# Attention in one visit of TensorE per pair of query blocks, with PSUM banks shared out by hand, in a hybrid decoder layer

## The chip, the core and the metric

The kernel runs on one NeuronCore of a Trainium2 chip. The metric is the device time of one execution in microseconds (us), start to end, as the median of several runs. The profile is one execution taken by the hardware profiler; its span reaches from the first to the last instruction of the core. In the profile PE is TensorE, PEld its weight loads, DVE is VectorE, ACT is ScalarE, POOL is GpSimd and SP the engine that issues most DMAs.

## The reference, cut to what matters

One decoder layer on x of 1024 tokens by 1024 features in float32: RMSNorm and one input projection; mixer A, a gated DeltaNet with 4 heads of 128; mixer B, dilated sliding-window attention with 8 heads of 64; an output projection with a residual; RMSNorm and a gated MLP of width 2816 with a short causal convolution; a last RMSNorm. The change is in mixer B and in what runs beside it. Each query sees three sets of keys, and the three softmaxes are merged by their denominators:

```
for window, dil in ((128, 1), (512, 4), (2048, 16)):     # keys t, t-dil, ..., t-window
    num, den, m = band_attention(stride(q), stride(k), stride(v), window // dil)
...
out = sum(exp(m_i - m_all) * num_i) / sum(exp(m_i - m_all) * den_i)
```

## The kernel before, in words

Everything is kept with features on partitions. A matrix product of the layer is done in three float32r products per 128-row step (`mm3`, L203), high part times high, high times low, low times high, so every weight and activation is cast to a high part on ScalarE (`whi`, `xhi`, `ohi`) and its rest is subtracted on VectorE (`wlo`, `xlo`, `olo`).

TensorE's order is made while the kernel is being built. The class `Weave` (L46) holds a list of Python generators, each a stream of work with a level; a generator yields the time for which its next product isn't ready by a model of engine times (`wv.need`, L95), and `Weave.run` (L102) always steps the stream of the lowest level whose time has come. The products get that order by a token (L190 to L201), so TensorE executes it strictly. The order on VectorE and ScalarE is made by a scheduler, which lets the operations through `uv` and `ua` (L151) go ahead of others; it too is fixed before the kernel runs. A product that waits for a bank or an operand therefore holds up all that stands behind it on TensorE.

The streams around the change are these. `dense` (L505) computes the input projection, column block by column block, each in two halves of 512 tokens; a half is 24 products of 128x512 that accumulate in one PSUM bank (`bank("hf")`, L525), and VectorE then scales it out of the bank (`scaled`, L444, into `aqkv` or `xr`). It has the last level and so fills what the others leave. The columns named `a` (queries, keys and values of attention, in four pairs of heads `pi`) go out to DRAM and are loaded again by `att_load` (L877); the columns `z` are gates, which `gate` (L481, `zz` and `og`) applies to the output of mixer A. `out_proj` (L1117) is the output projection, `mixer_splits` (L1089) the casts of its input `ots`.

`attention` (L906) takes a pair of heads at a time, in two groups (`hh`) of four query blocks of 128 tokens. Its unit is a pair of blocks (`u` = 0 and 2, each block an `it`). A block has near keys (its own and the previous block) and, from block 2 on, far keys in four classes by position modulo 4 (`far`, 32 columns per block further back). The steps of a pair are:

- `scores` (L917): per block and head of the pair, one product with the near keys and four small ones with the far keys of the classes. The first block writes the two banks `asc`, the second the two banks `atr`.
- `softmax` and `normalise` (L941): a masked minimum on VectorE, the exponential on ScalarE, a reciprocal and a multiplication on VectorE; the result is `sm`.
- `turn` (L983): transposes of `sm` in halves of 64 rows (`tp_half`, L198), again into `asc` for the first and `atr` for the second block; `turned` (L962) copies them out, the near part on VectorE (`pt`), the far part on ScalarE (`pb`).
- `values` (L1002): products of `pt` with the values, into the bank `po` of the group, one of the two banks `ch`.
- after the second pair of a group, `merge_classes` (L1011): products of `pb` with the values sorted by class, also into `po`; `give` (L1025) copies `po` out (`oT`) on VectorE.

`advance` (L1040) runs these in a pipeline one pair deep: it turns the pair before, then does the scores of the next pair, then the values of the pair before (and its classes). Each of `turn`, `scores`, `values` and `merge_classes` begins with its own `yield`, so that other streams may be placed ahead of it. When `att_values` (L883, transposes of the values of the next head pair) is due, it stands between `turn` and `scores`.

[...] `bank` (L253) draws from four tags of two: `hf`, `atr`, `asc`, `ch`; a tile of a tag waits until the tile two before it has been read by all its readers.

Of the kernel before, what the change touches and what calls it, by code (L numbers as in the profile page):

```python
# [15 lines left out]
P = 128  # L16
# [128 lines left out]
def hybrid_layer(tc, I, out):  # L145
# [16 lines left out]
    pp_ = es.enter_context(tc.tile_pool(name="pp", bufs=2, space=PSUM))  # L162
# [89 lines left out]

    def bank(tag, name="ps"):  # L253
        return tile_(pp_, (P, 512), F32, name, tag, 2)

    def next_bank(tag, *tiles, slack=0.0):

        while max(wv.need(*tiles), wv.slot_free(tag, 2)) + slack > 1e-3:
            yield max(wv.need(*tiles), wv.slot_free(tag, 2)) + slack
        return bank(tag)  # L260
# [218 lines left out]
    put_off = []  # L479

# [24 lines left out]
    def dense():  # L505
# [400 lines left out]
    def attention():  # L906
# [10 lines left out]
        def scores(pair):  # L917

            for it, tag in zip(pair, ("asc", "atr")):
# [4 lines left out]
            yield wv.need(*pair[0]["ps"], *pair[1]["ps"], pair[0]["q"], pair[0]["k"])  # L924
# [37 lines left out]
        def turned(it, h, pts, b, pp):  # L962
# [5 lines left out]
            if it["g"]["pi"] == 3 and it["n"] == 7 and h == 1:  # L968
# [13 lines left out]

        def turn(pair):  # L983
            def wait():

                return max(wv.need(pair[0]["sm"]) + TSLACK[0], *[wv.slot_free(t, n) for t in ("asc", "atr")
                                                                 for n in (1, 2)])
            while wait() > 1e-3:
                yield wait()
# [12 lines left out]
        def values(pair):  # L1002
            yield wv.need(pair[0]["po"], *pair[0]["pt"], slack=-PSLACK)
            for it in pair:
                u = it["u"]
                for i in range(it["n1"] // P):
                    for e, er in enumerate(HALVES):
                        mm(it["po"][er, u * P:(u + 1) * P], v8(it["vn"])[:, it["k0"] // P + i, er],
                           it["pt"][e][:, i * P:(i + 1) * P], 0.11, u == 0 and i == 0, False, skip_group_check=True)
# [30 lines left out]
        def advance(pair, more=None):  # L1040
            done = pipe.pop() if pipe else None
            if done is not None:
                yield from turn(done)
            if more is not None:
                last["values"] = yield from more
            if pair is not None:
                yield from scores(pair)
                pipe.append(pair)
            if done is not None:
                yield from values(done)  # L1050
                if done[1]["u"] == 3:
                    yield from merge_classes(done[0]["g"])
                    give(done[0]["g"])

        for pi in range(4):
            q, k, vn, vc = cur
            for hh in range(2):
# [4 lines left out]
                po = bank("ch")  # L1062
# [6 lines left out]
                g = dict(po=po, pb=pb, nb=nb, hh=hh, pi=pi, vc=vc)  # L1069
                for u in (0, 2):  # L1070
                    more = att_values(qkv[2]) if (hh, u) == (1, 2) and pi < 3 else None
                    yield from advance([dict(n=4 * hh + i, u=i, q=q, k=k, vn=vn, far=32 * max(4 * hh + i - 1, 0), po=po, pb=pb, g=g)
# [3 lines left out]
        yield from advance(None)  # L1076
        wv.done.add("attention")
# [39 lines left out]
    def out_proj():  # L1117
# [6 lines left out]
        todo = [(k, j) for k in range(8) for j in range(2)]  # L1124
        while todo:

            now = [a for a in todo if ("ot", a[0]) in wv.done and (a[1] == 0 or "attention" in wv.done)]
# [3 lines left out]
            k, j = now[0]  # L1131
# [7 lines left out]
            if m not in pts:  # L1139
                pts[m] = [bank(("hf", "ch")[j]) for _ in range(2)]  # L1140
            for h in range(2):
                yield wv.need(pts[m][h], *w, *ots[k])
                mm3(pts[m][h], [t[:, k, :] for t in w], [t[:, half(h)] for t in ots[k]], k == 0, k == 7)
        for j, m in enumerate(MORDER):
            w = ws.pop(0)
            for h in range(2):
# [6 lines left out]
                else:  # L1153
                    pt = pts[m][h]
# [612 lines left out]
```

## Time and profile before

| | us |
|---|---|
| runs, median of 3 (lowest to highest) | 1205.56 (1205.49 to 1207.72) |
| profiled execution, span on the core | 1204.1 |
| median of the runs above that span | 1.46 |
| mean granted TensorE clock | 0.998 |
| attention, from the first scores to the last class values | 308.0 to 463.3 |

The page's part 1 gives busy time per engine and part 4 the chain of work that ended last. A timeline row has the start, the length, the engine and line, and the operation with its tiles, and xN where N like instructions in a row are merged; a float32 product counts as two. Matmuls are pipelined, so lengths of neighbours overlap, and the cost of a step is read from start to start. A windows row has the stretch, its length, then busy time and count for PE, PEld, DVE, ACT and POOL, the granted clock, the DMA share and GB/s. A group row has the total busy time, the mean in ns, and the idle time in front with what ended it. Lines are those of the kernel before; L139 and L141 are the helpers through which VectorE and ScalarE operations are recorded.

### The profile page before, as it was taken

What the parts mean: (1) busy time and instruction counts of PE and PEld (TensorE: products, weight loads), DVE (VectorE), ACT (ScalarE), POOL (GpSimd) and SP (SyncE); (2) the same over time, 40 slices, a digit from 0 to 9 for tenths busy, and PEclk for the clock granted to TensorE, in tenths of its full rate; (3) what the DMA queues carried; (4) which work ended last, traced back from release to release, by engine and by line L of the source; (5) the groups of instructions that cost most, each with busy time, mean ns of one, the idle gap of its engine ahead of it and who ended that gap; (6) DMA issues with size and microseconds to landing.
All of it is one profiled execution on the core that took longest, in us unless ns stands there. A gap on an engine that the chain in (4) does not pass through costs nothing.

```text
span 1204.1 us, 18360 instructions
## 1 busy us (share of the span) xinstructions
PE 1194.7 (99%) x7058; PEld 987.9 (82%) x7058; DVE 957.1 (79%) x1530; ACT 575.9 (48%) x1131; POOL 54.3 (5%) x50
## 2 busy tenths in 40 slices
PE   9999999999999999999999999999999999999997
PEld 7888887898777777888888888888888888888887
DVE  7686985474667687767898989889898889898987
ACT  7383344364444444555554544444454454445452
POOL 0212110023000000000000000000000000000001
PEclk9999999999999999999999999999999999999999
DMA  7323234426433323443123132231322296357734
GB/s 236 106 75 102 77 119 122 157 79 212 166 115 106 106 63 123 150 140 140 56 85 106 59 100 89 69 105 53 105 71 86 94 370 227 109 179 223 242 97 157
DMA packets 81704, 152.72 MB, mean 127 GB/s; under 512 B 21552, under 2 KB 32592, under 8 KB 81616
## 3 DMA queue, kind: packets, MB, share of 16 engines
q1 hardware_dynamic: 80896, 151.02, 38.3%
q8 instruction: 55, 0.90, 0.3%
q10 hardware_dynamic: 720, 0.53, 0.1%
q14 instruction: 33, 0.27, 0.1%
HBM read 113.49 MB, written 35.93 MB: 124 GB/s over the span
## 4 chain that ended last, share of the span: by engine, by line
PE 98%; DVE 1%; ACT 0%; issue 0%; POOL 0%; DVEq 0%; ACTq 0%; POOLq 0%
PE ps L191 48%; PE pa L191 20%; PE dw L191 17%; PE pc L191 10%; PE ps L195 2%; PE ps L200 1%; PE warm L191 0%; DVE x1h L139 0%; ACT sm L141 0%; PE pd L191 0%; DVE sm L141 0%; POOL rs L139 0%; DVE xr L139 0%; ACT u L139 0%; ACT sq L139 0%
## 5 line engine op out<-in xcount | busy, mean ns | idle before, releaser
L191 PE MATMUL dw<-pr 128*128 128x512 f32 (+1 forms) x984 | 211.4, 377 | 0.0
L191 PEld LDWEIGHTS dw<-pr 128*128 128x128 f32 x984 | 176.8, 188 | 33.5
L191 PE MATMUL ps<-xhi,whi 128*128 128x512 f32 x448 | 186.4, 416 | 0.0
L191 PE MATMUL ps<-xhi,wlo 128*128 128x512 f32 x448 | 175.8, 392 | 0.0
L191 PE MATMUL ps<-xlo,whi 128*128 128x512 f32 x448 | 175.4, 391 | 0.0
L191 PE MATMUL pa<-T,pair 128*128 128x512 f32 x528 | 127.1, 390 | 0.1
L191 PEld LDWEIGHTS pa<-T,pair 128*128 128x128 f32 x528 | 99.0, 188 | 20.9 <-ACT u L139 0.5
L191 PEld LDWEIGHTS ps<-xhi,whi 128*128 128x128 f32 x448 | 84.7, 189 | 19.4 <-issue 2.7
L191 PEld LDWEIGHTS ps<-xhi,wlo 128*128 128x128 f32 x448 | 84.3, 188 | 18.4
L191 PEld LDWEIGHTS ps<-xlo,whi 128*128 128x128 f32 x448 | 84.9, 189 | 13.7
L139 ACT ACTIVATE u<-pa 128x512 f32<-128x512 f32 x44 | 26.3, 599 | 109.7 <-PE pa L191 109.7
L139 DVE SCALAR_TENSOR_TENSOR y<-xu,fcw,y 128x1023 f32<-128x1023 f32 (+1 forms) x44 | 56.4, 1281 | 24.4 <-ACT y L139 24.4
L139 ACT ACTIVATE pr<-wd 128x1024 fp32r<-128x1024 f32 x33 | 35.0, 1061 | 73.9 <-DVE wd L139 36.9
L139 ACT ACTIVATE whi<-wst 128x1024 fp32r<-128x1024 f32 (+2 forms) x38 | 38.6, 1015 | 62.7 <-PE ps L191 55.7
L191 PE MATMUL pa<-B,A 128*128 128x512 f32 x264 | 63.5, 390 | 0.0
L191 PE MATMUL pa<-T,S 128*128 128x512 f32 x264 | 63.4, 390 | 0.0
L191 PE MATMUL pc<-T,S 128*128 128x512 f32 x264 | 63.4, 390 | 0.0
L191 PE MATMUL pc<-B,pair 128*128 128x512 f32 x264 | 63.4, 390 | 0.0
L139 DVE TENSOR_TENSOR wst<-wst 128x512 f32<-128x512 f32 x88 | 60.5, 687 | 0.8
L191 PE MATMUL ps<-B,pair 128*128 128x512 f32 x252 | 60.6, 390 | 0.0
L141 ACT ACTIVATE sm<-sm,mx 128x128 f32<-128x128 f32 (+7 forms) x64 | 35.5, 555 | 48.1 <-DVE mx L141 48.1
L191 PEld LDWEIGHTS pa<-T,S 128*128 128x128 f32 x264 | 49.6, 188 | 10.2
(240 smaller groups left out, 2253.1 us busy)
## 6 DMA issues: line engine op xcount, KB each, us to landing
wst<-in_wu SPq DMA_DIRECT2D x44, 512.0 KB, 3.7
wd<-in_wd SPq DMA_DIRECT2D x44, 512.0 KB, 4.5
wst<-in_wi SPq DMA_DIRECT2D x25, 512.0 KB, 3.7
upark<-y SPq DMA_DIRECT2D x22, 512.0 KB, 3.7
r<-upark SPq DMA_DIRECT2D x22, 512.0 KB, 10.2
apark<-aqkv SPq DMA_DIRECT2D x12, 512.0 KB, 3.0
wa<-in_wd SPq DMA_DIRECT2D x22, 256.0 KB, 3.0
wst<-in_wo SPq DMA_DIRECT2D x8, 512.0 KB, 3.8
```

Source lines behind the costliest of these rows:

```text
L139: return getattr(eng, op)(*a, **kw)
L141: return getattr(eng, op)(*a, **kw)
L191: tc.stamp_issue_order_token(nc.tensor.matmul(dst, lhs, rhs, start=start, stop=stop, **kw).ins, TOKEN)
L195: tc.stamp_issue_order_token(nc.tensor.transpose(dst, src, ident).ins, TOKEN)
L200: tc.stamp_issue_order_token(nc.tensor.transpose(dst, src[rows], ident[rows, rows]).ins, TOKEN)
```

## The change

The steps of attention lose their own yields. `ready` waits once ahead of a visit for the softmax of the pair before, for the banks `asc` and `atr`, for the next queries and for `ch`; then turning, next scores, values and classes are placed with nothing between them, and `att_values` comes after the visit. The scores of the first block go to `ch` and of the second to `asc`; the turning keeps `asc` and `atr`. From the start of attention one of the two `hf` banks is `po`, for all groups, and the dense halves alternate between the other `hf` bank and the first `ch` bank (`dense_bank`); no visit is placed while a dense half in that `ch` bank is unfinished (`shared`). At the end of attention `hf` has two banks again, and the next one drawn is the second. `out_proj` works off its first products per half (`h`), and before attention ends only those of the first half of the first output block may be placed.

```diff
+    BANKS = {t: [t + "0", t + "1"] for t in ("hf", "atr", "asc", "ch")}
+    taken = {t: 0 for t in BANKS}
     def bank(tag, name="ps"):
-        return tile_(pp_, (P, 512), F32, name, tag, 2)
+        ring = BANKS[tag]
+        taken[tag] += 1
+        return tile_(pp_, (P, 512), F32, name, ring[(taken[tag] - 1) % len(ring)], 1)
+    def bank_free(tag, n=1):
+        ring = BANKS[tag]
+        return max(wv.slot_free(ring[(taken[tag] + i) % len(ring)], 1) for i in range(n))
...
+    shared, turns_of = [False], [0]
+    def dense_bank():
+        if BANKS["hf"] != ["hf0"]:
+            return bank("hf")
+        turns_of[0] += 1
+        shared[0] = turns_of[0] % 2 == 0
+        return tile_(pp_, (P, 512), F32, "ps", "ch0", 1) if shared[0] else bank("hf")
...
-                pt = bank("hf")
+                pt = dense_bank()
...
+                shared[0] = False
...
-            for it, tag in zip(pair, ("asc", "atr")):
+            for it, tag in zip(pair, ("ch", "asc")):
...
-            yield wv.need(*pair[0]["ps"], *pair[1]["ps"], pair[0]["q"], pair[0]["k"])
...
-            if it["g"]["pi"] == 3 and it["n"] == 7 and h == 1:
+            if it["g"]["pi"] == 3 and it["n"] == 7 and h == 1 and "dense" in wv.done:
...
+        def ready(done, pair):
+            def wait():
+                t = [0.0]
+                if done is not None:
+                    t += [wv.need(done[0]["sm"]) + TSLACK[0], wv.need(done[1]["sm"]) + TSLACK[1],
+                          bank_free("asc", 2), bank_free("atr", 2)]
+                if pair is not None:
+                    t += [wv.need(pair[0]["q"], pair[0]["k"]), bank_free("ch", 2) - (0.7 if done is not None else 0.0)]
+                    if done is None:
+                        t.append(bank_free("asc", 2))
+                return max(t)
+            while wait() > 1e-3 or shared[0]:
+                yield max(wait(), 0.1)
...
         def values(pair):
-            yield wv.need(pair[0]["po"], *pair[0]["pt"], slack=-PSLACK)
+            g = pair[0]["g"]
+            if "po" not in g:
+                g["po"] = bank("po")
...
         def merge_classes(g):
-            yield wv.need(*g["pb"], slack=-PSLACK)
...
         def advance(pair, more=None):
             done = pipe.pop() if pipe else None
+            yield from ready(done, pair)
             if done is not None:
-                yield from turn(done)
-            if more is not None:
-                last["values"] = yield from more
+                turn(done)
             if pair is not None:
-                yield from scores(pair)
+                scores(pair)
                 pipe.append(pair)
             if done is not None:
-                yield from values(done)
+                values(done)
                 if done[1]["u"] == 3:
-                    yield from merge_classes(done[0]["g"])
+                    merge_classes(done[0]["g"])
                     give(done[0]["g"])
+            if more is not None:
+                yield 0.3
+                last["values"] = yield from more
+        BANKS["hf"], BANKS["po"] = ["hf0"], ["hf1"]
+        taken["po"] = 0
...
-                po = bank("ch")
...
         yield from advance(None)
+        BANKS["hf"], taken["hf"] = ["hf0", "hf1"], 1
         wv.done.add("attention")
...
-        todo = [(k, j) for k in range(8) for j in range(2)]
+        todo = [(k, j, h) for k in range(8) for j in range(2) for h in range(2)]
...
-            now = [a for a in todo if ("ot", a[0]) in wv.done and (a[1] == 0 or "attention" in wv.done)]
+            now = [a for a in todo if ("ot", a[0]) in wv.done and (a[1:] == (0, 0) or "attention" in wv.done)]
...
-            if m not in pts:
-                pts[m] = [bank(("hf", "ch")[j]) for _ in range(2)]
+            if (m, h) not in pts:
+                pts[m, h] = bank(("hf", "ch")[j])
```

More of the change, by code (lines that the diff above doesn't have):

```diff
@@ L981, in far_blocks @@
             return [min(4, it["far"] // 32 - 4 * b) for b in range(-(-it["far"] // P))]
-        def turn(pair):
[L984 to L989, printed above, removed]
+        def ready(done, pair):
[11 more added lines that the diff above has]
+                yield max(wait(), 0.1)
+        def turn(pair):
             pts = A("pt", "dv*", shape=(P, 4, 256))
@@ L1068, in attention @@
                     wv.done.add("last group")
-                g = dict(po=po, pb=pb, nb=nb, hh=hh, pi=pi, vc=vc)
+                g = dict(pb=pb, nb=nb, hh=hh, pi=pi, vc=vc)
                 for u in (0, 2):
                     more = att_values(qkv[2]) if (hh, u) == (1, 2) and pi < 3 else None
-                    yield from advance([dict(n=4 * hh + i, u=i, q=q, k=k, vn=vn, far=32 * max(4 * hh + i - 1, 0), po=po, pb=pb, g=g)
+                    yield from advance([dict(n=4 * hh + i, u=i, q=q, k=k, vn=vn, far=32 * max(4 * hh + i - 1, 0), pb=pb, g=g)
                                         for i in (u, u + 1)], more)
@@ L1130, in out_proj @@
                 continue
-            k, j = now[0]
+            k, j, h = now[0]
             todo.remove(now[0])
@@ L1138, in out_proj @@
                 split(raw_weight(I["wo"][MORDER[2]]), *third)
-            if m not in pts:
-                pts[m] = [bank(("hf", "ch")[j]) for _ in range(2)]
-            for h in range(2):
-                yield wv.need(pts[m][h], *w, *ots[k])
-                mm3(pts[m][h], [t[:, k, :] for t in w], [t[:, half(h)] for t in ots[k]], k == 0, k == 7)
+            if (m, h) not in pts:
+                pts[m, h] = bank(("hf", "ch")[j])
+            yield wv.need(pts[m, h], *w, *ots[k])
+            mm3(pts[m, h], [t[:, k, :] for t in w], [t[:, half(h)] for t in ots[k]], k == 0, k == 7)
         for j, m in enumerate(MORDER):
@@ L1153, in out_proj @@
                 else:
-                    pt = pts[m][h]
+                    pt = pts[m, h]
                 ve.tensor_tensor(x1[m][:, half(h)], x1[m][:, half(h)], pt, op=OP.add)
```

8 lines of the change are left out of this document (4 added, 4 removed).

## The prediction

> **What bounds the kernel now.** I read the page's shares first, then its chain of work, then the busy times of the attention stretch beside those of a plain stretch.
>
> ```profile
> PE 1194.7 (99%) x7058; PEld 987.9 (82%) x7058; DVE 957.1 (79%) x1530; ACT 575.9 (48%) x1131; POOL 54.3 (5%) x50
> ...
> PE 98%; DVE 1%; ACT 0%; issue 0%; POOL 0%; DVEq 0%; ACTq 0%; POOLq 0%
> ```
>
> TensorE (PE) is the whole chain. Next, stretches by busy time: attention first, then a stretch of MLP.
>
> ```profile
> 305.77:463.29 157.52, 157.37 (x1727) 121.48 (x1725) 109.71 (x324) 67.89 (x212) 3.65 (x8) 1.00 0.32 103
> 700.00:800.00 100.00, 100.00 (x443) 82.89 (x442) 88.67 (x103) 47.73 (x64) 0.00 (x0) 1.00 0.24 79
> ```
>
> PE never idles in attention: dense products fill every wait. A plain product costs 100/443 = 0.226 us. So only two things can change the time: work or emptying that TensorE no longer does, and waits that it now meets in its own queue with nothing placed before them. VectorE's 109.7 us of 157.5 leave slack on average, not at each moment.
>
> **The change, part by part.** In the profile a turning is L200 sm (T), scores are kT,qT (S), values pt,vn (V), class values pb,vc (C). Before, T and S of one step stand apart with dense products between.
>
> ```profile
> 358.55 0.96 PE L200 MATMUL ps<-ident,sm 64*128 64x64 f32 x24
> 359.44 0.50 PE L191 MATMUL ps<-xhi,whi 128*128 128x512 f32 x1
> ...
> 361.70 1.68 PE L191 MATMUL ps<-kT,qT 64*128 64x256 f32 x40
> ...
> 342.90 1.22 PE L200 MATMUL ps<-ident,sm 64*128 64x64 f32 x32
> 344.04 0.50 PE L191 MATMUL ps<-xhi,whi 128*128 128x512 f32 x1
> ...
> 346.32 0.93 PE L191 MATMUL ps<-kT,qT 64*128 64x128 f32 x8
> 347.18 1.09 PE L191 MATMUL ps<-pt,vn 128*64 128x128 f32 x16
> 348.10 1.51 PE L191 MATMUL ps<-pb,vc 128*64 128x128 f32 x32
> 349.54 0.97 PE L200 MATMUL ps<-ident,sm 64*128 64x64 f32 x12
> ```
>
> Start to start, 24 transposes take 0.89 us, 32 take 1.14 (0.031 each); a short S (blocks 0 and 1) takes 0.86, V 0.92, and the long C 1.44.
>
> *Gain.* From T at 358.55 to S at 361.70 are 3.15 us. Nine products (2.03) and 24 transposes (0.74) explain 2.77; **0.38 us is the price of parting T from S**. It goes if S can follow T with no gap; a T followed directly by S is not in the trace, so the gain is 0 to 0.38. I take 0.33, near the upper end, because T and S load weights of one shape:
>
> ```profile
> 358.54 0.82 PEld L200 LDWEIGHTS ps<-ident,sm 64*128 64x128 f32 x24 [0.35 <-issue]
> ...
> 361.70 0.73 PEld L191 LDWEIGHTS ps<-kT,qT 64*128 64x128 f32 x8 [0.35 <-ACT pb L141]
> ```
>
> The loader idles 0.35 us at each entry from 128-row products into this 64-row shape. [...]
>
> The order of the changed program's instructions shows 16 partings gone (15 T–S, one T–V) and three new ones, where a T now comes apart from the C before it: 16 × 0.33 − 3 × 0.25 = 4.5 us. Three turnings also waited for probabilities:
>
> ```profile
> PEld ps L200 <- DVE sm L141: 0.8, 3, 0.4
> ```
>
> In the changed order 18 or more products stand ahead of a turning, save two places (six and nine). Gain: 4.5 + 0.8 = **5.3 us** (0.8 to 6.2).
>
> *Loss 1, a bank used twice running.* From attention's start "hf" is one bank, hf0, and dense halves alternate between hf0 and ch0. The half in hand at that moment lies in hf0, and the next one again takes hf0. So its first product waits until VectorE has scaled the half just finished. The nearest rows are the last (24th) product of an earlier half and its scaling:
>
> ```profile
> 303.39 0.39 PE L191 MATMUL ps<-xhi,wlo 128*128 128x512 f32 x1
> ...
> 303.82 1.13 DVE L139 TENSOR_TENSOR aqkv<-ps,rstdB 128x512 f32<-128x512 f32 x1 [5.27 <-PE ps L191]
> ```
>
> 0.43 to its start, 1.1 to its end, 0.07 to hand over: 1.6 us where 0.23 was needed. **+1.4 us.** VectorE is free then (bounds 1.2 to 1.7).
>
> *Loss 2, asc inside a visit.* T of a pair's first block writes the two asc banks, and S of the next pair's second block now writes the same two, 0.5 us later in TensorE's own order. It must wait until VectorE has copied the near part (pt) and ScalarE the far part (pb). Before, nine products (2 us) covered that. Unhindered rows:
>
> ```profile
> 367.75 0.96 PE L200 MATMUL ps<-ident,sm 64*128 64x64 f32 x24
> ...
> 368.37 1.42 DVE L141 COPY pt<-ps 128x256 f32<-128x256 f32 x4 [0.50 <-PE ps L200]
> 368.88 1.21 ACT L141 ACTIVATE pb<-ps 96x128 f32<-96x128 f32 x4 [2.54 <-DVE pt L141]
> ```
>
> Copies run at +0.62 us from T's start, one each 0.33; the second pb ends at 1.13 + 0.31 + 0.28 = 1.72. TensorE reaches the fourth local score at 0.89 + 3 × 0.18 = 1.44 (eight loads take 0.73). Wait: 0.28 plus handing over, 0.33. Eight visits (those that turn blocks 2, 3 or 4, 5) pay it: **2.6 us**. The four that turn blocks 0 and 1 have no pb: 0.05 each, **0.2**. Behind the waiting S stand V, C and all dense products. Bounds 0 to 0.6 a visit.
>
> *Loss 3, three visits that turn blocks 6 and 7 ahead of a next pair.* In two of them the program puts on VectorE, right at T, the scaling of the dense half that has just ended, then two copies, then a wlo subtraction, then two copies. Costs:
>
> ```profile
> L139 DVE TENSOR_TENSOR wlo<-wst,whi 128x1024 fp32r<-128x1024 f32 (+2 forms) x38 | 45.5, 1199 | 8.8 <-ACT whi L139 8.6
> ...
> 382.56 1.40 DVE L141 COPY pt<-ps 128x256 f32<-128x256 f32 x4
> 383.00 1.42 ACT L141 ACTIVATE pb<-ps 128x128 f32<-128x128 f32 x8 [2.43 <-DVE pt L141]
> ```
>
> Scaling ends at 1.07, the copies at 1.75, wlo at 2.9, the other copies at 3.6. V's second half would start at 1.14 + 0.86 + 0.46 = 2.46 and starts at 3.65: 1.2 each, 2.4. The third has VectorE free: the second bank is cleared at 2.05 rather than 1.54, 0.5. **+2.9 us** (1 to 4).
>
> *Loss 4, the end of attention.* Count from S of the last pair (blocks 6, 7).
>
> ```profile
> 451.71 1.89 PE L191 MATMUL ps<-kT,qT 64*128 64x256 f32 x40
> 454.56 0.50 PE L191 MATMUL ps<-xhi,whi 128*128 128x512 f32 x1
> ...
> 453.37 0.59 DVE L141 CUSTOM_DVE_ANT_0 sm<-ps,mk 128x416 f32<-128x416 f32 x1 [2.10 <-PE ps L191]
> ...
> 456.96 0.82 DVE L141 TENSOR_SCALAR sm<-sm,mx 128x448 f32<-128x448 f32 x2
> 457.70 0.68 DVE L139 TENSOR_TENSOR xr<-ps,rstdB 128x512 f32<-128x512 f32 x1
> ```
>
> S and V take 2.85. Only nine dense products are left before the last T (15 now), so TensorE turns at 0.33 + 2.85 + 2.3 = 5.45 and with T, V and C (3.5) would be done at 8.95. But the first output product behind takes the second "hf" bank, which is the po bank: it waits for oT, the copy that empties po. In VectorE's order oT stands behind the softmax (ends 6.1 + 0.33 = 6.4), xr (7.0), four copies (8.4), two wlo, olo, zz and another olo, and only then itself.
>
> ```profile
> L139 DVE TENSOR_TENSOR olo<-og,ohi 128x1024 fp32r<-128x1024 f32 x4 | 4.7, 1222 | 1.4 <-ACT ohi L139 1.4
> L139 DVE SCALAR_TENSOR_TENSOR zz<-zz,xr 128x1024 f32<-128x1024 f32 x4 | 4.9, 1222 | 1.1 <-ACT zz L139 1.1
> L139 DVE COPY oT<-ps 128x512 f32<-128x512 f32 x8 | 8.5, 1057 | 0.0
> ...
> L139 ACT ACTIVATE zz<-xr 128x1024 f32<-128x1024 f32 x4 | 4.2, 1047 | 0.7 <-DVE og L139 0.7
> L139 ACT ACTIVATE ohi<-og 128x1024 fp32r<-128x1024 f32 x4 | 4.0, 1053 | 5.8 <-PE ps L191 3.1 <-DVE og L139 2.7
> ```
>
> Five at 1.15 start to start give 14.1, oT 15.2, the product 15.3 instead of 9.0: **+6.4 us** (3 to 7). Inside it ScalarE puts zz ahead of all pb copies and an ohi cast between them (7.1 + 1.05 + 0.7 + 1.0 + 0.7), so C starts near 10.5 and the hole falls in two parts, 1.6 before C and 3.2 behind it.
>
> *Loss 5, the clock.* Only the kernel's edges show what a hole does:
>
> ```profile
> 1198.00:1200.00 2.00, 0.04 (x1) 0.00 (x0) 2.00 (x6) 0.38 (x1) 1.40 (x2) 0.59 0.56 183
> ...
> 1.10 4.64 PE L191 MATMUL warm<-warm 128*128 128x128 f32 x20 [1.10 <-DVE ones L139]
> ...
> 6.39 0.63 PE L191 MATMUL ps<-xhi,wlo 128*128 128x512 f32 x1
> ...
> 7.20 0.40 PE L191 MATMUL ps<-xlo,whi 128*128 128x512 f32 x1
> ```
>
> The granted clock falls to 0.59 over the two us behind TensorE's last work; at the start, with work from 1.1 us on, products take 0.63, and 0.40 only from 7.2 us. The price is 0 (no fall) to 3 (those six us at half speed); I take the middle, **1.5 us**. [...]
>
> The po bank itself, one instead of two, costs nothing elsewhere: 18 or more products lie between C and the next V, save one place with six, where oT is next on VectorE. ch0 as a dense bank costs nothing: its scaling ends 0.4 us into the T that stands before S. PE's instructions are the same in kind and number; no DMA is added, and the loads of the next queries are issued earlier or alike.
>
> **Sum.** −5.3 + 1.4 + 2.6 + 0.2 + 2.9 + 6.4 + 1.5 = +9.7 us. Against the profiled span of 1204.1 this is 1213.8; the median of the runs, 1205.56, stands 1.46 above that span (start and end lie outside it), so the forecast is **1215.3 us**.
>
> **Rivals.**
> 1. *VectorE and ScalarE are ahead*: the banks are empty when TensorE arrives, inside the visits and at the end, because copies start sooner than +0.62 and the late queue has drained. Losses 2 to 5 vanish and the gain is whole: 1205.56 − 6.2 + 1.4 = 1200.8, faster. It decides once all waits together fall below about 3 us. For it: VectorE's mean share, 70% of the stretch. Against: the copies' start is a row, and the orders are fixed.
> 2. *The end is not paid*: oT comes as C ends, losses 4 and 5 fall away: 1205.56 − 5.3 + 7.1 = 1207.4. For it: before, oT ran soon after C. Against: five long instructions stand ahead.
> 3. *S needs its own emptying behind T*, as S's two parts and V do, and the clock falls: gain 16 × 0.1 − 0.75 + 0.8 = 1.6, losses 2 to 4 and 1 as above with 1.5 to 3 for the clock, 15.0 to 16.5: 1219.0 to 1220.5. Against: one load shape.
> 4. That the change doesn't do what it says is excluded by the order: 16 visits, none with dense products inside.
>
> **How the numbers follow.** Forecast 0.70, rival 1 0.06, rival 2 0.11, rival 3 0.13. A measurement of this kernel tells about 0.2% (2.4 us) from no change. Faster, below 1203.2: rival 1, 0.06. Within: rival 2, 0.11. Slower: 0.83. The forecast's own bounds, with losses 2 to 4 at half their spread, are ±5; the range 1208.5 to 1220.5 leaves out rivals 1 and 2 and a little of 3.
>
> **What would show it.** Right: waits of PE (loader rows) on ACT pb or DVE pt of about 0.3 in each visit, one wait on aqkv of 1.4 near attention's start, one on oT of about 3 at its end, with the clock under 1.00 behind it; T to S start to start at 0.75 to 0.9 for 24 transposes plus that wait. Wrong: PE at 157 of 157 through attention, or a first output product that waits for nothing.

## The result, and the profile after

The changed kernel takes **1217.9 us** (median of four runs, 1216.33 to 1218.18) against 1205.5 of the kernel before on the same chip: a ratio of 1.0096, 95% interval 1.0084 to 1.0108. It is slower by about 1%: its fastest run lies above the slowest of the kernel before (1207.72). The forecast was 1215.3 in a range of 1208.5 to 1220.5. The profiled execution is the one of 1216.33; its span is 1214.5 against 1204.1 before, 10.4 us more. The other three runs are 1.5 to 1.9 longer at a slightly lower mean granted clock (0.994 to 0.995 instead of 0.997); the first experiment shows what such a difference can be. So of the 2.6 us by which the median exceeds the forecast, 0.7 lie in the profiled span and the rest between the runs.

The page of the changed kernel, busy time and chain, and its waits of TensorE (columns: total us, times, longest):

```profile
PE 1197.6 (99%) x7058; PEld 989.6 (81%) x7058; DVE 957.4 (79%) x1530; ACT 575.2 (47%) x1131; POOL 54.2 (4%) x50
...
PE 96%; DVE 2%; DMA 1%; ACT 1%; issue 0%; POOL 0%; DVEq 0%; ACTq 0%; POOLq 0%
```

```profile
PE ps L191 <- DVE oT L139: 3.5, 1, 3.5
PE ps L191 <- ACT pb L141: 2.1, 4, 0.9
PE ps L191 <- DVE aqkv L139: 1.1, 1, 1.1
...
PE ps L191 <- DVE pt L141: 0.8, 1, 0.8
```

The instructions of TensorE are the same in number (x7058). The chain is no longer PE alone: VectorE and ScalarE have entered it, by four releasers that TensorE did not wait for before: oT, pb, aqkv and pt. They are the releasers of losses 1 to 4. But the list counts only time in which PE stands still, and a product whose weights come late is counted as busy. So I measure steps start to start, from one kind of product to the next.

The end of attention, TensorE and then VectorE:

```profile
471.99 1.48 PE L200 MATMUL ps<-ident,sm 64*128 64x64 f32 x32
474.27 1.32 PE L191 MATMUL ps<-pt,vn 128*64 128x128 f32 x16 [0.80 <-DVE pt L141]
476.52 1.56 PE L191 MATMUL ps<-pb,vc 128*64 128x128 f32 x32 [0.93 <-ACT pb L141]
481.57 0.50 PE L191 MATMUL ps<-ohi,whi 128*128 128x512 f32 x1 [3.49 <-DVE oT L139]
...
483.21 0.63 PE L191 MATMUL ps<-ohi,whi 128*128 128x512 f32 x1
```

```profile
472.87 0.68 DVE L139 TENSOR_TENSOR xr<-ps,rstdB 128x512 f32<-128x512 f32 x1
473.47 1.41 DVE L141 COPY pt<-ps 128x256 f32<-128x256 f32 x4
474.79 2.35 DVE L139 TENSOR_TENSOR wlo<-wst,whi 128x1024 fp32r<-128x1024 f32 x2
477.06 1.22 DVE L139 TENSOR_TENSOR olo<-og,ohi 128x1024 fp32r<-128x1024 f32 x1
...
480.47 1.05 DVE L139 COPY oT<-ps 128x512 f32<-128x512 f32 x1
```

T, V and C take 9.58 us from 471.99 to 481.57 instead of 3.50, in three holes, and oT comes last in VectorE's line as foreseen. The clock falls behind it. The windows of after, with PEclk as the third number from the end of each row:

```profile
480.00:482.00 2.00, 0.43 (x2) 0.39 (x3) 2.00 (x3) 0.72 (x1) 0.00 (x0) 1.00 0.86 293
482.00:484.00 2.00, 2.00 (x8) 1.60 (x7) 2.00 (x3) 1.40 (x2) 0.00 (x0) 0.72 0.87 290
484.00:486.00 2.00, 2.00 (x6) 1.55 (x5) 2.00 (x3) 0.72 (x3) 0.00 (x0) 0.50 0.93 313
486.00:488.00 2.00, 2.00 (x9) 1.60 (x9) 0.81 (x2) 0.98 (x2) 0.00 (x0) 0.93 0.84 323
```

Inside attention, a visit that turns blocks 2 and 3, and one that turns blocks 6 and 7 (TensorE; of the second also VectorE):

```profile
319.86 0.96 PE L200 MATMUL ps<-ident,sm 64*128 64x64 f32 x24
320.66 2.17 PE L191 MATMUL ps<-kT,qT 64*128 64x256 f32 x40
322.76 0.44 PE L191 MATMUL ps<-pt,vn 128*64 128x128 f32 x4
...
341.26 1.22 PE L200 MATMUL ps<-ident,sm 64*128 64x64 f32 x32
342.32 0.44 PE L191 MATMUL ps<-kT,qT 64*128 64x128 f32 x4
343.25 1.02 PE L191 MATMUL ps<-kT,qT 64*128 64x256 f32 x4 [0.49 <-ACT pb L141]
344.20 1.37 PE L191 MATMUL ps<-pt,vn 128*64 128x128 f32 x16
345.40 1.51 PE L191 MATMUL ps<-pb,vc 128*64 128x128 f32 x32
```

```profile
341.37 1.11 DVE L139 TENSOR_TENSOR aqkv<-ps,rstdB 128x512 f32<-128x512 f32 x1 [2.76 <-PE ps L191]
342.32 0.73 DVE L141 COPY pt<-ps 128x256 f32<-128x256 f32 x2
342.98 1.22 DVE L139 TENSOR_TENSOR wlo<-wst,whi 128x1024 fp32r<-128x1024 f32 x1
344.11 0.75 DVE L141 COPY pt<-ps 128x256 f32<-128x256 f32 x2
```

S follows T with no gap: 24 transposes take 0.80 start to start. But S of blocks 4, 5 takes 2.10 (320.66 to 322.76) where it took 1.61 alone, and TensorE's own row shows no idle time. The row of its weight loads does: the first four of eight loads start at 320.60, and the other four wait for a pb copy, with no change of shape there.

```profile
321.25 0.63 PEld L191 LDWEIGHTS ps<-kT,qT 64*128 64x128 f32 x4 [0.35 <-ACT pb L141]
```

To compare kernels without what the clock does later, I use one **mark**: the start of the first group of products behind the output projection.

```profile
580.57 1.84 PE L191 MATMUL ps<-ones,rstdB 128*128 128x1 f32 x16
```

In the kernel before the same row stands at 570.23. So 10.3 of the 10.4 us have arisen by there. The first S of attention, ahead of which no experiment edits an order, starts between 306.05 and 306.95 in the kernels below, so a mark alone is good to about half a us; where a few tenths matter, the rows of the visits decide.

### The profile page after: what moved, and what is told of

It reads as the page before. It is cut to its first block, busy times and chain, and to the rows that moved or that the text cites. A ratio compares the mean times of both kernels' runs of the same rounds, so it can differ in the third digit from the quotient of the medians.

```text
span 1214.5 us, 18341 instructions
## 1 busy us (share of the span) xinstructions
PE 1197.6 (99%) x7058; PEld 989.6 (81%) x7058; DVE 957.4 (79%) x1530; ACT 575.2 (47%) x1131; POOL 54.2 (4%) x50
## 4 chain that ended last, share of the span: by engine, by line
PE 96%; DVE 2%; DMA 1%; ACT 1%; issue 0%; POOL 0%; DVEq 0%; ACTq 0%; POOLq 0%
PE ps L191 47%; PE pa L191 19%; PE dw L191 17%; PE pc L191 10%; PE ps L195 2%; PE ps L200 1%; DMA wst<-in_wu 0%; DVE wlo L139 0%; DVE pt L141 0%; PE warm L191 0%; DVE x1h L139 0%; DMA wst<-in_wo 0%; DVE aqkv L139 0%; DVE T L139 0%; DVE wst L139 0%
## 5 line engine op out<-in xcount | busy, mean ns | idle before, releaser
L191 PEld LDWEIGHTS pc<-T,S 128*128 128x128 f32 x264 | 49.5, 188 | 10.3
L191 PEld LDWEIGHTS pa<-T,S 128*128 128x128 f32 x264 | 49.5, 188 | 10.3
```

Source lines behind the costliest of these rows:

```text
L191: tc.stamp_issue_order_token(nc.tensor.matmul(dst, lhs, rhs, start=start, stop=stop, **kw).ins, TOKEN)
```

## The experiments

The theory: merging gains about 5 us and the waits for banks in TensorE's own queue cost some 15. Rivals: the merged visit costs by itself (changes of shape with nothing between), or the layout of the banks costs with or without the visit. Each time is given with its ratio to runs of the kernel before on the same chip.

### 1. Copies ahead of wlo

```diff
-                    turned(it, h, pts, b, pps[h])
+                    copied = turned(it, h, pts, b, pps[h])
+            if it["g"]["pi"] < 3 and "dense" not in wv.done:
+                after(lows_made[-1], copied, "the probabilities go first")
```

> The wlo subtractions of attention's weights are put behind the four pt copies of a visit; nothing else is asked for. Theory (loss 3: in two visits V waits for the copies of the second block, which stand behind a wlo): V no longer starts late there, two visits at 1.2 us, so 1217.9 - 2.4 = 1215.5 (1214.9 to 1216.4), and the visits at 341 and 382 us shorten from 5.58 to about 4.4 from the turning to the next dense product. Rival (the visits are long because TensorE empties at each change of shape, and VectorE's order does not matter): 1217.9, same lengths.

Measured: 1216.8, ratio 1.0085 (1.0071 to 1.0099); mark 579.15. The visit at 341 us:

```profile
342.77 0.44 PE L191 MATMUL ps<-kT,qT 64*128 64x128 f32 x4
343.71 1.02 PE L191 MATMUL ps<-kT,qT 64*128 64x256 f32 x4 [0.49 <-ACT pb L141]
344.66 1.09 PE L191 MATMUL ps<-pt,vn 128*64 128x128 f32 x16
345.58 1.51 PE L191 MATMUL ps<-pb,vc 128*64 128x128 f32 x32
```

V to C is 0.92 again instead of 1.20, but S to V still 1.89. The wlo cost 0.28 a visit, not 1.2; the rest of loss 3 is S, which waits for asc. The theory's place was wrong here.

This profile also has two spells of half clock, and neither begins behind a hole like the one of 3.49 us in the changed kernel. The first begins at the start of C, behind holes of 0.80 (before V) and 0.93 (before C); ahead of the second the longest wait is 0.28:

```profile
476.00:478.00 2.00, 1.30 (x16) 1.33 (x18) 2.00 (x3) 1.03 (x5) 0.00 (x0) 0.67 0.43 84
478.00:480.00 2.00, 1.53 (x22) 1.34 (x18) 2.00 (x3) 0.20 (x1) 0.00 (x0) 0.50 0.80 285
...
580.00:582.00 2.00, 1.72 (x12) 1.55 (x13) 1.87 (x4) 1.90 (x4) 0.00 (x0) 1.00 0.00 0
582.00:584.00 2.00, 2.00 (x7) 1.55 (x7) 2.00 (x6) 1.79 (x3) 1.00 (x1) 0.62 0.00 0
584.00:586.00 2.00, 2.00 (x7) 1.55 (x6) 1.80 (x3) 0.16 (x1) 0.95 (x1) 0.53 0.00 0
```

The first falls into C and the wait for oT that follows, and costs nothing: from C to the first output product are 5.05 us, as in the changed kernel. That kernel's own spell behind the hole (1.6) is absent here; this and the wlo (0.6) make the earlier mark. The second lies at the norm, which the change doesn't touch, and costs about 1.7 us: the distance to the mark's place before is 8.9, and 1.8 more by the end. That is the size by which the runs of one kernel differ from each other.

### 2. The first shared half in ch0

```diff
-    shared, turns_of = [False], [0]
+    shared, turns_of = [False], [1]
```

> As the run with the copies first, and the first dense half that starts in attention takes ch0 instead of hf0, so that no bank is used twice running. Theory (loss 1): the wait of 1.4 us on the scaling (aqkv) near 311 us goes: 1.4 below the run with the copies first, 1214.1 (1213.3 to 1214.9). Rival (VectorE is late there whatever the bank, so the wait moves to the next half): no difference, 1215.5.

Measured: 1216.2, ratio 1.0076 (1.0063 to 1.0090); mark 580.78. The wait on aqkv is gone: the stretch of dense products ahead of the first T is longer than 0.2257 each by 0.28 instead of 1.67, so loss 1 is 1.4 as predicted. The time gained only 0.6 on experiment 1, because the other grid of halves moves the last visits (S of blocks 6, 7 at the end 3.12 instead of 2.32) and the half clock lasted 6.8 us here. Confirmed in its place, not in the total.

### 3. Other banks for the first output products

```diff
-        BANKS["hf"], taken["hf"] = ["hf0", "hf1"], 1
+        BANKS["hf"], taken["hf"] = ["hf0", "hf1"], 0
...
-                pts[m, h] = bank(("hf", "ch")[j])
+                pts[m, h] = bank(("ch", "hf")[j])
```

> The changed kernel, but the first output products draw the banks ch0, ch1, hf0 and only the fourth group of three draws hf1 (the po bank, emptied by oT); the orders of all engines stay. Theory (loss 4, and 5 as its consequence): nine products of 0.226 cover 2.0 us of the wait for oT, so the hole falls from 3.5 to about 1.5 us: -1.9, and if the clock falls only behind a long hole, another -1.6: 1214.4 to 1216.0. Rival A (VectorE's late queue is the limit: the products would wait for olo and wlo instead, which stand in the same queue): 1217 to 1218 with the wait renamed. Rival B (the clock falls for any hole of a microsecond): 1216.0 with the window of half clock still there.

Measured: 1213.5, ratio 1.0060 (1.0047 to 1.0073), 0.9 below the expected range; mark 577.26, 3.3 earlier than the changed kernel.

```profile
479.86 0.39 PE L191 MATMUL ps<-ohi,wlo 128*128 128x512 f32 x1
481.48 0.50 PE L191 MATMUL ps<-ohi,whi 128*128 128x512 f32 x1 [1.23 <-DVE oT L139]
```

Nine products run before oT is needed, the hole falls from 3.49 to 1.23, and the granted clock is 1.00 in every window behind it (mean clock 0.998, as in the kernel before). Rival A falls: the weights were not late. Rival B falls for this execution, in which holes of 0.8, 0.9 and 1.2 did not drop the clock; it does not fall altogether, since in experiment 1 the clock dropped behind holes of 0.8 and 0.9, and the four other runs here have a lower mean clock (0.995 to 0.997 instead of 0.998). This run and experiment 9 are the cleanest, since the orders of all engines stay.

### 4. T and S parted again

```diff
             if pair is not None:
+                if done is not None:
+                    yield 0.1
+                    yield from ready(None, pair)
                 scores(pair)
                 pipe.append(pair)
             if done is not None:
+                yield wv.need(*done[0]["pt"], slack=-PSLACK)
                 values(done)
                 if done[1]["u"] == 3:
+                    yield wv.need(*done[0]["g"]["pb"], slack=-PSLACK)
                     merge_classes(done[0]["g"])
```

> The changed kernel with its banks and its end, but T and S parted again: S waits its turn in the plan until the banks that T wrote are free, so dense products stand between T and S; V and C are also planned by their operands. Theory: the partings come back (15 at 0.33, +5.0) and the waits inside the visits go (asc: measured 8 x 0.49 = -3.9 and 4 x 0.05; second copies: -2.6), the end stays: 1217.9 + 5.0 - 4.1 - 2.6 = 1216.2 (1214.5 to 1218). Rival A (the merged visit itself costs, by changes of shape without products between): about 1208 to 1210. Rival B (merging gains far more than 0.33 a visit and the banks alone cost): 1220 and more.

Measured: 1238.0, ratio 1.0261 (1.0247 to 1.0275). Far outside what either side expected, and not for their reasons:

```profile
PE ps L200 <- DVE sm L141: 10.8, 7, 3.3
PE ps L191 <- DVE pt L141: 6.9, 2, 6.3
```

A visit may begin or go on only when no dense half lies in ch0. Parted, S comes later, its softmax misses the next such moment, and visits come 48 dense products apart (42 and 6). The dense products run out, and the last visits wait with nothing before them. As a test of the gain it is void. It shows what the visit does for the plan: with these banks, parting is not free to choose. So the rival that the layout costs without the visit too is not refuted. What the rows do show, in the visits that still had dense products to part T and S: S takes 0.86, 1.40, 1.61 and 1.82, as in the kernel before, so its longer times in the changed kernel belong to S standing right behind T.

### 5. Eight visits parted by three products

```diff
             if pair is not None:
+                if done is not None and done[1]["n"] in (1, 5):
+                    yield 0.05
+                    while shared[0]:
+                        yield 0.1
                 scores(pair)
```

> The changed kernel, but in eight of the sixteen visits (those that turn blocks 0 and 1 or 4 and 5) one step of three dense products stands between T and S, and the scores wait for a free bank by the plan; the number of dense products behind attention stays. Theory: each parting costs 0.35 (two changes of shape with the loader idle) and its three products (0.68) cover the wait on asc inside: 0.50 in four of the eight, 0.05 in the others. 8 x 0.35 - 2.2 + 0.7 (the last stretch is three products shorter, so the end's hole grows) = +1.3: 1219.2 (1218 to 1220), and S of blocks 6 and 7 runs 1.82 again instead of 2.32. Rival A (a merged visit costs by itself): below 1217. Rival B (a parting costs much more than 0.35, and merging was the whole gain): above 1221.

Measured: 1221.3, ratio 1.0126 (1.0112 to 1.0140).

```profile
336.12 0.96 PE L200 MATMUL ps<-ident,sm 64*128 64x64 f32 x24
337.01 0.50 PE L191 MATMUL ps<-xhi,whi 128*128 128x512 f32 x1
...
337.90 1.89 PE L191 MATMUL ps<-kT,qT 64*128 64x256 f32 x40
339.72 1.09 PE L191 MATMUL ps<-pt,vn 128*64 128x128 f32 x16
...
PE ps L191 <- DVE mx L141: 2.7, 2, 1.5
```

The time is that of rival B, the rows are not. T takes 0.89 instead of 0.80, the three products 0.89 instead of 0.68, so a parting costs 0.09 + 0.21 = 0.30; and S of blocks 6 and 7 takes 1.82, its wait gone. The surplus is 2.7 us in which dense products wait for the softmax (mx) to have read ch0, a longer hole for oT (4.7), and a spell of half clock of 6.8 us instead of 3.4 (mean clock 0.995, as in experiment 2). So my forecast of this run failed by a wait that I had not counted, while the price of a parting stands.

### 6. Copies ahead of the scaling

```diff
+                if copies:
+                    after(inst, copies.pop(), "the probabilities go first")   # inst: the aqkv scaling
```

> As the run with the copies first, and in the two visits at 341 and 382 us the scaling (aqkv) of the dense half just ended goes behind the pt copies too. Theory, corrected after the first runs: what is left of loss 3 there is the wait of S on asc, 0.94 instead of 0.05, because the copies start 0.47 us later behind the 1.1 us scaling: 5.30 to about 4.7 per visit, -1.2 in all: 1215.6 (1215.0 to 1216.4). Rival (ScalarE's pb copies, and not VectorE's order, set the wait): no difference, 1216.8.

Measured: 1216.9, ratio 1.0089 (1.0076 to 1.0103); mark 580.17. The time says nothing; the rows do: S to V in the two visits 1.59 instead of 1.89, half of what was expected. 0.73 is left above the bare S of 0.86, with the copies starting at once. That part is the wait for asc itself. It is longer than elsewhere because block 6 has two far parts per bank, so that two more pb copies stand in the chain. By the trace of this run the second pb of the first bank ends at 343.56 and S goes on at 343.61; the second pb of the other bank ends at 343.89 and S goes on at 343.93.

### 7. Far parts first

```diff
+            near(a)
+            distant(a)
+            distant(b)
+            near(b)
```

`near` and `distant` are the two loops of `scores`, each made a function of one block.

> As the run before it, and S computes the near part of the first block, both far parts, then the near part of the second block, so that asc is wanted about 1 us later. Theory (loss 2: eight waits of 0.49 on the copies out of asc): they go, and one more change between the shapes of near and far part is paid in 12 visits, 0 to 0.2 each: -3.9 + 0 to 2.4, so 1.5 to 3.9 below the run before, 1212 to 1214. Rival (the 0.49 is a change of shape inside S and no wait for a bank): not faster, 1215.6 to 1218.

Measured: 1217.4, ratio 1.0094 (1.0081 to 1.0108). The theory's gain did not come. S of blocks 2, 3, which hardly waited, rises from 1.40 to 1.60: one more change between the shapes of the near and the far products costs 0.2. Against the bare S plus this 0.2 (1.81 for blocks 4, 5 and 2.02 for 6, 7), five of the eight waiting visits are nearly bare, S 1.94 twice and 2.05 three times (332.30 to 334.36), so there the wait went as expected. In the other three S takes 2.36, 2.34 and 2.58. The plan had moved: 21 dense products instead of 18 stand ahead of these three, so that the copies come behind the scaling of a half, or, in the third, pb behind a gate's zz on ScalarE.

```profile
332.30 2.12 PE L191 MATMUL ps<-kT,qT 64*128 64x256 f32 x40
334.36 1.09 PE L191 MATMUL ps<-pt,vn 128*64 128x128 f32 x16
```

The first of the three, whose T starts at 320.52, on VectorE:

```profile
320.62 1.11 DVE L139 TENSOR_TENSOR aqkv<-ps,rstdB 128x512 f32<-128x512 f32 x1 [2.66 <-PE ps L191]
321.57 1.40 DVE L141 COPY pt<-ps 128x256 f32<-128x256 f32 x4
```

So what was saved in waits was paid in changes of shape and in three later copies; the hole for oT is longer too (4.67), and the half clock lasted 6.8 us. The time is the rival's, the rows are not: in the five visits S became shorter although one more change of shape lies inside it.

### 8. All remedies so far

The edits of 1, 2, 3, 6 and 7 together, and oT ahead of zz and the later olo.

> All remedies together: copies ahead of wlo and scaling, far parts first, first half in ch0, first output products in ch and hf0, oT ahead of zz and the later olo. Theory (the change is a gain of about 5 us with 15 us of waits on top): nearly all waits go: 1205.5 - 5.3 + what stays (0 to 2.4 for the shape change, up to 1 at the end): 1200.5 to 1204, below the kernel before. Rival (merging gains nothing, the waits are all there is): 1205.5 to 1208.

Measured: 1210.4, ratio 1.0037 (1.0023 to 1.0050); mark 574.24. Neither theory nor rival. Summed from the rows, S still takes 30.0 us in all against 22.9 before, and T, V and C at the end 1.8 more than bare: the waits were not out. That sent me to the chain of copies itself.

### 9. Two copiers side by side

```diff
+            first = h == 1 and len(far_blocks(it)) == 1
+            if first:
+                far_copies()
             inst = uv.tensor_copy(...)
-            for i, n_ in enumerate(far_blocks(it)):
-                ua.activation(...)
+            if not first:
+                far_copies()
```

`far_copies` holds the loop that is taken out below it.

> The changed kernel, but for blocks 2 to 5 ScalarE empties the far part (pb) of a block's second bank before VectorE takes its near part (pt), so that the two engines work on the two banks at the same time instead of one behind the other; the order on each engine stays. Theory (loss 2: S waits for the chain of copies out of asc, pt of bank 1, pt of bank 2 beside pb of bank 1, pb of bank 2): the chain is one copy shorter, 0.3 us, so S of blocks 4, 5 falls from 2.10 to about 1.8 and S of blocks 6, 7 from 2.32 to about 2.0, eight times 0.3: -2.4, 1215.5 (1215.0 to 1216.3). Rival (the extra time in S is a drain behind T and no bank): S stays at 2.10 and 2.32, 1217.9.

Measured: 1215.0, ratio 1.0074 (1.0061 to 1.0086); mark 579.24. The visit that was shown above:

```profile
320.60 0.96 PE L200 MATMUL ps<-ident,sm 64*128 64x64 f32 x24
321.39 1.88 PE L191 MATMUL ps<-kT,qT 64*128 64x256 f32 x40
323.20 0.98 PE L191 MATMUL ps<-pt,vn 128*64 128x128 f32 x14
```

S takes 1.80 to 1.87 instead of 2.10, and 2.03 to 2.09 instead of 2.32 for blocks 6, 7: 2.0 us in the eight visits, of 2.4 expected. (The mark moved by 1.3, with the first S 0.7 later.) No engine's order changed, so the extra time in S is the wait for the copies, though TensorE's row shows no idle time there. The rival falls: it had S stay at 2.10 and 2.32.

### 10. All remedies, two copiers instead of far parts first

> All remedies, with the copies of the two banks side by side in place of the far parts first, and the copies ahead of wlo to the end of attention. From the rows of the run with all waits out (4.3 us longer than the kernel before up to its last transpose): far parts first is given up (S 5.98 to 5.82 for three visits, -0.6 in all), S of blocks 4, 5 and 6, 7 falls by 0.3 each (-2.4), the waits behind wlo in the last visits go (-1.5). 1210.4 - 4.5 = 1205.9 (1204.5 to 1208), level with the kernel before. If the merged visit gained more than the partings it removes, it would be below 1204; if the waits are not in the copies, above 1208.

Measured: 1207.8, ratio 1.0015 (1.0006 to 1.0024); mark 572.01. At the upper end of what was expected: the waits behind wlo did not go in two late visits (S 2.29 and 2.82), where og, xr and another wlo stand ahead of the copies.

### 11. Short scores in one pair of banks

```diff
-                it["ps"] = [bank(tag) for _ in range(2)]
+                if it["n"] == 1:
+                    it["ps"] = [p[:, P:3 * P] for p in pair[0]["ps"]]
+                else:
+                    it["ps"] = [bank(tag) for _ in range(2)]
```

and the copies ahead of og, wlo, xr, the last tanh and the last ohi.

> As the best run so far (1207.8, its last products 1.8 us behind those of the kernel before), with two more remedies. (1) The short scores of blocks 0 and 1 both go into the two ch banks (128 + 256 of 512 columns each), so this S no longer needs asc: 1.58 to 0.86, three times 0.72: -2.2. (2) In the last three visits the copies go ahead of og, wlo, xr, the last tanh and the last ohi: S of 2.29 and 2.82 to 1.85 and 2.09, V at the end from 2.22 to about 1.2, T from 1.55 to 1.3: -2.4. Theory (all added time is banks that TensorE waits for in its own queue): 1207.8 - 4.6 = 1203.2 (1202 to 1205), below the kernel before. Rival (the waits move to the next resource, VectorE's late softmax or weights): 1206 to 1208.

Measured: 1205.8, ratio 1.0002 (0.9993 to 1.0011); mark 569.69. This lies between the theory's range and the rival's. S of blocks 0, 1 is 0.80, which is bare, and the last V 1.15. The mark is 0.5 ahead of the kernel before; two new waits of 0.57 for ch0, which the softmax reads late, and one of 0.7 for oT had come in.

### 12. Two orders mended

Scaling before the copies again in two visits, oT ahead of the third olo.

> As the run with the short scores in one pair, less two waits that its rows show: (1) in two visits the scaling (aqkv) goes ahead of the copies again, since S there no longer needs asc, so the softmax empties ch0 before the next dense half draws it: C to next product 2.01 to about 1.5, twice 0.5; (2) oT goes ahead of the third olo, which removes the wait of 0.7 on oT. Theory: 1205.8 - 1.7 = 1204.1 (1203.3 to 1205), a little below the kernel before. Rival: as quick as the run before it, 1205.8.

Measured: **1204.2**, ratio 0.9987 (0.9978 to 0.9996).

```profile
568.04 1.84 PE L191 MATMUL ps<-ones,rstdB 128*128 128x1 f32 x16
```

The mark is 2.2 ahead of the kernel before, 12.5 ahead of the changed one. It is the only version below both: 0.13% below the kernel before, with 0.9996 as the interval's upper end. No run gives the kernel before the same new orders and banks, so how much of this merging alone is worth isn't shown by a time; the rows of T (1.9 less) and of the dense stretches (3.0 less, both below) price it.

## Why the prediction was right, point by point

The direction and the size were right, and the places but for that of loss 3: +9.7 forecast, +10.4 in the profiled span. By its steps:

| step | predicted | measured in the rows of after |
|---|---|---|
| gain, net of three new partings | -5.3 | -4.9 |
| loss 1, hf0 twice running | +1.4 | +1.4 |
| loss 2, asc inside the visit | +2.8 | +4.1 |
| loss 3, three visits that turn 6, 7 | +2.9 | +3.1, in another place |
| loss 4, end of attention | +6.4 | +6.1 |
| loss 5, clock | +1.5 | +1.6 |

The right column sums to 11.4, 1.0 more than the spans differ. Ahead of attention 0.4 of that is found: the changed kernel's first S comes 1.8 earlier, with six products fewer (1.4) before it. Behind attention 0.7 is found: in the kernel before, the loads of two output products wait for xr (0.53, at 473.21) and for wlo (0.46, at 474.66), which costs 0.7 start to start, and the changed kernel has no such waits. Neither was in the prediction. So part of the nearness is luck: the steps together came out 1.7 higher than summed, and these two places gave 1.1 back.

**Gain.** A merged T of 24 is 0.09 shorter (0.80 for 0.89) and a stretch of dense products less saves 0.23 to 0.25 over its 0.2257 each: 0.33, as taken. The stretches between the first S and the last C fall from 32 to 19, which saves 3.0; the T save 1.9, of which 0.7 are the waits for probabilities, which did go. Experiment 5 bought a parting back for 0.30. Rival 3 (a price of S behind T) is refuted: 0.80 is less than any T of 24 before, and S of blocks 2, 3 right behind T takes 1.40 in two visits, as before. The weight loads of the first visit shown agree: they idle 0.35 us ahead of T, 0.33 between the near and the far products of S and 0.20 ahead of V, and not at all between T and S. Experiment 7 gives the price of one more change inside S: 0.2.

**Loss 1.** Right in mechanism, place and size (1.67 - 0.24; experiment 2 removes it).

**Loss 2.** The mechanism was right and the size was not. The step that was mis-sized is the wait of 0.33: it measured 0.49 in blocks 4, 5 and 0.50 in 6, 7, inside the "bounds 0 to 0.6 a visit". The copies kept the times of the sum (in the first visit shown, T starts at 319.86, pt at 320.48, pb at 320.94), but S reached asc 0.09 earlier, behind a T with no gap; the other 0.07 I put down to the restart of the products, which is argued and not shown. The foreseen sign, a wait of the loads for pb of about 0.3, is the loader's row above (0.35). Experiment 9 shows that it is the chain of copies, pt of the first bank, pt of the second, pb of the second: with one link less S is 0.3 shorter.

**Loss 3.** "V's second half would start at 2.46 and starts at 3.65: 1.2 each" is the step that failed, though the sum was within 0.2. The rows show V 0.28 longer and S 1.02 longer. I had applied loss 2 to these visits only where the third pays 0.5. But the wait for asc applies to all three, with a longer chain of copies than in the others, and the scaling holds the copies for 0.3 more. Experiments 1 and 6 part the three causes: wlo 0.28, scaling 0.30, asc 0.73; experiment 11 takes the asc part to nothing. With S late, V was late anyway, and the wlo was hidden behind it.

**Loss 4.** Right in its total and in what comes last, from the last S at 466.38: T at +5.61 (5.45 foreseen), C at +10.14 (10.5), the first product at +15.19 (15.3). But the prediction split the wait in two, 1.6 before C and 3.2 behind it, and it fell in three: 0.80 before V, which waits for pt, 0.93 before C and 3.49 behind it. Experiment 3 takes 2.3 of it by the banks alone.

**Loss 5.** 1.6 in this execution: eight products 0.38 to 0.43 apart instead of 0.23. The upper price of the forecast, 3, did not fall due here; experiments 2 and 7, with the hole as long or longer, had a spell of twice the length, 6.8 us. The other three runs of the changed kernel are 1.5 to 1.9 longer at a mean clock lower by 0.002 to 0.003; that is 2.4 to 3.6 us of lost clock, an estimate from their 1216 us, so the higher price, or a second spell, fell due there, though no profile shows where. The middle was a choice between two lengths, not a size, and that it fitted the profiled execution is luck.

**ch0 costs nothing** held for the changed kernel; in experiments 5 and 11 dense products waited 2.7 and 1.0 us for the softmax to have read ch0.

**Rival 2** ("the end is not paid") is what experiment 3 partly makes true, and the time then is 1213.5, not 1207.4. That sum had the waits inside attention in it already. What is left is at the end: the other banks take 2.3 of 6.1, and the holes before V and C and 1.2 us of waiting for oT stay; loss 2 is 1.3 larger as well. **Rival 1** (no waits, 1200.8) is refuted for the changed kernel, where every wait came. It is where experiment 12 goes: with the waits gone but some 3 us (2.0 in S, 0.6 in V, 0.5 in the last T), it reads 1204.2.

## What to carry to other kernels

Fill between two steps of an in-order engine is not only waste: it covers the copies that free the banks between them. Before taking it out, list for each bank who writes it next in that engine's own order, how many copies must end before, and what stands ahead of these copies on theirs. A saved parting (0.33 here) is worth no more than one copy for which TensorE then has to wait (0.3 here), and the last use of a buffer before a phase ends deserves a place in front of the other engines' queues.

## What the runs showed of the hardware

- **The half clock came in spells of 3.4 us or of twice that.** In after it lasts about 3.4 us (0.50 between 484 and 486, with 0.72 and 0.93 in the windows before and behind), in experiment 1 twice about 3.4, in experiments 2 and 7 about 6.8, and in experiment 5 as well, with the same mean clock of 0.995. It began at different points of the work: 1.3 us after work had resumed (after), within the hole (experiment 2, where the clock falls at 479.6 and work resumes at 480.74; experiment 7, 480 and 481.83), at the start of C behind two short holes (experiment 1, 476.68, by the 0.67 of 476 to 478), or in the middle of work (experiment 1, 582.48, by the 0.62 of 582 to 584). This last spell follows a stretch in which PE was busy 1.72 of 2 us, half of it with products of one column, and the longest wait before it was 0.28. What sets the beginning and the length is not shown.
- **A wait need not show as idle time of TensorE.** S of 40 products with a wait of 0.49 inside is one row of 2.17 busy us without a bracket, because products overlap (the dense ones are 0.39 long and 0.23 apart in the rows) and their ends are modelled. The weight loads show 0.35 of it. Start to start is the measure.
- **Copies of VectorE and ScalarE out of one bank ran one behind the other** (in the first visit shown of after, pb started 0.46 behind pt, with pt as its releaser); out of two banks they ran at once (in experiment 9 pt started at 321.22 and pb at 321.25). The releaser means that the program made pb wait; no run shows what the chip would do without that.
- **Changing the shape of products had a price here:** 0.30 (experiment 5) to 0.33 us (after against before) for a stretch of 128-row products between T and S, 0.2 for one more change between the near and the far products of S (experiment 7, 1.60 for 1.40), and nothing between T and S (in after T of 24 takes 0.80, and S of blocks 2, 3 takes 1.40 as before).
